# Idle products ahead of the first weights, an earlier split of the first weight, and three modulation steps taken behind the recurrence

## The chip, the cores and the metric

The kernel runs on one core of one Trainium2 chip. The metric is device microseconds (us) of one execution. The kernel before takes 2224.59 us, the median of 3 runs (2222.05 to 2225.04).

## What is computed

Two blocks of layers on 256 tokens, in fp32, with D = 1024. The first has an RG-LRU layer, a convolutional feed-forward, a stick-breaking attention and a second feed-forward, each followed by a layer norm:

```python
def rg_lru_block(x, w_in, b_in, conv_w, conv_b, w_gates, b_gates, a_param, w_out, b_out):
    proj = x @ w_in + b_in
    y_br = jax.nn.gelu(proj[..., :LRU_WIDTH])
    x_br = causal_depthwise_conv(proj[..., LRU_WIDTH:], conv_w, conv_b)
    ...
    _, h = lax.associative_scan(_lin_combine, (a, u), axis=1)
    return (h.astype(x.dtype) * y_br) @ w_out + b_out
...
        x = layer_norm(DN_ALPHA * x + mix, ln_g[layer, 0], ln_b[layer, 0])
        f = conv_ffn(x, ffn_w_up[layer], ffn_conv_w[layer], ffn_conv_b[layer], ffn_w_down[layer])
        x = layer_norm(DN_ALPHA * x + f, ln_g[layer, 1], ln_b[layer, 1])
```

The second block takes tokens and context through a Fourier and convolution mixer, attentions and two mixtures of experts, and ends in a norm. Its norms are scaled and shifted by a modulation that depends on neither block's tokens: silu(c) @ mod_w for two vectors c, of 6144 columns per layer and two layers. So the modulation can be computed at any time before the mixer.

## The kernel before

Activations lie transposed, 128 features on the partitions and eight chunks of 256 tokens behind each other. All weights stream from memory through a ring of 1 MB tiles (five of them in the first block), by DMAs that SyncE (SP) issues in the order of use (`start` and `load` in `run`); a tile's slot is free for the next when both of its halves have been used.

An fp32 product is made of three in a faster format. A weight piece is split by `cut`: ScalarE (ACT) copies it to `wh` (L382), VectorE (DVE) makes the rest `wl = w - wh` (L383). The tokens are split likewise into `xh` and `xl` (`parts`, in `begin` of `_first_block`: four quarters, L396 on ACT). TensorE (PE) then runs 8 x 3 products of 128 by 256 per piece: `wh` with `xh` (L405), `wh` with `xl` (L406), `wl` with `xh` (L407). Pieces are split up to four ahead of their products (`SPLITS`); a step of kind "ahead", which `K.ahead(n)` adds, makes the loop split up to n pieces beyond those already used.

The program is a list of steps that `run` carries out in order; each engine's queue has its instructions in that order. In `_lru` the order is: four pairs of signal products with the convolution behind them (`signal`, taps on DVE and GpSimd, POOL), with the small DVE instructions of `rates` (L711 to L730) behind the first pair; gates; four pairs of branch products with `decay`, `recur` (the scan) and `finish` between them. `finish(q)` is, for a quarter of the features, the Gelu (`yb`, L802, ACT), its product with the scan's result (`gi`, L806, DVE), and the split of that into `xbh` (L807, ACT) and `xbl` (L813, DVE). Behind `finish(3)` comes the output projection (`_block_out`, four pairs, accumulators `acc`), whose sums DVE adds to x (L692), and then the first layer norm: four centrings (DVE, L507, 512 columns each), their squares (ACT, L551) and column sums (PE, L564), the sum read by ACT (L571), a root, four scalings.

Two lists of steps wait at the side, a heavy one and a light one. `fill()` stands at numbered spots of the program, and takes from each list as many steps as the digit of `HEAVY` or `LIGHT` at that spot says, as far as there are any. Spot 2 is between the third pair with `finish(1)`, `finish(2)` and `finish(3)`; 4 to 7 lie in the output projection, 8 to 17 in the first layer norm (before it, after each centring, the root and each scaling), 18 to 53 in the first feed-forward, 54 to 63 in the second layer norm, and from 142 on in the mixer.

The light list holds the 48 modulation steps (`_modulation`, `one(g, k)`), each with a weight tile of 1 MB of its own, `mod_w`, used unsplit. A step is four products (L1082; eight records in the trace). The first step also sets up `sc`, silu of the two vectors (a memset on DVE, two Silus on ACT, L1076 and L1077). Every eighth step ends a group: a copy from PSUM on ACT (L1086), four transposes on PE (L1089), two additions on DVE (L1093). `LIGHT` has 48 in all.

`warm(n)` issues n products of 128 by 256 in bf16 whose result nobody reads.

Of the kernel before, what the change touches and what calls it, by code (L numbers as in the profile page):

```python
# [21 lines left out]
KC = D // P  # L22
# [131 lines left out]
class _K:  # L154
# [126 lines left out]
    def fill(self):  # L281

        for kind, table in ((self.heavy, HEAVY), (self.light, LIGHT)):
            n = int(table[self.spot]) if self.spot < len(table) else 0
# [110 lines left out]
    def parts(self, h, l, src):  # L395
        self.nc.scalar.activation(h, src, AF.Copy)  # L396
        self.nc.vector.tensor_sub(l, src, h)
# [57 lines left out]
            v.scalar_tensor_tensor(y, w, b, y, op0=ALU.add, op1=ALU.mult)  # L455
        return y

    def warm(self, n):

        w = self.cst[:, :256].bitcast(mybir.dt.bfloat16)  # L460
        ps = self.pt()[:, :w.shape[1]]
        for _ in range(n):
            self.nc.tensor.matmul(ps, lhsT=w[:, :P], rhs=w, start=True, stop=True)
# [76 lines left out]
class _Rms:  # L540
# [37 lines left out]
    def root(self, warm=0):  # L578
        ss = self.total() if self.ss is None else self.ss
        self.d = self.K.diagonal(self.K.inverse_root(ss[:, :, 0], [(2, self.n * P)], self.eps))  # L580
        self.K.warm(warm)
# [61 lines left out]


WARM = [8, 4, 4, 6]
HEAVY = "0000000000000100000000000000000000010101001000110000000000022001000001000000301000000010000000100001000100000000001000010000000000000000010000131301010000000000008110024100000000000"
LIGHT = "0000001101020010310001000110302000001010100100110100000500000000000000000100000000000000000100100000000000000000000000000000000000000001000011001001110000110000000001020300000000000"


class _Box:  # L650
# [392 lines left out]
def _first_block(K, X):  # L1043
    def begin():
        X.new("xh", [P, KC, T], F32R)
        X.new("xl", [P, KC, T], F32R)
        for q in range(0, KC, 2):
            K.parts(X.xh[:, q:q + 2], X.xl[:, q:q + 2], K.x[:, q:q + 2])
    K.add(begin)
    xh, xl, sy = (lambda: X.xh), (lambda: X.xl), (lambda: X.sy)  # L1050
    _lru(K, X)
    K.add(lambda: K.enter("cx", "right"))
    K.layer_norm(sy, 0, xh, xl)
    _ffn(K, 0, X)
    K.layer_norm(sy, 1, xh, xl)
    _stick(K, X)
    K.layer_norm(sy, 2, xh, xl)
    sums = _TwoNorms(K, 3)
    K.add(lambda: K.enter("two"))
    K.add(sums.prepare)  # L1060
    _ffn(K, 1, X)
    K.layer_norm(sy, 3, None, None, sums)
    K.add(lambda: K.leave("two"))
    return sums
# [37 lines left out]
def _modulate(K, src, l, r, which, gain, pool, parts=None, out=None, tmp=None, rms=None):  # L1102
# [10 lines left out]
    def first():  # L1113
# [3 lines left out]
        if summed:  # L1117
            rms.root(WARM[0])
            return
# [14 lines left out]
    def scale(k0):  # L1134
        def fn():
            if k0 == 0:
                box["r"] = rms.row()
                if summed:
                    K.warm(WARM[1])
            ks = range(k0, k0 + 4)  # L1140
# [532 lines left out]
class _Moe:  # L1673
# [87 lines left out]
    def experts(self, i, rms=None, side=None, tail=None):  # L1761
# [453 lines left out]
        self.tokens(i, "moe", ("xg", "yh"), keep=True, rms=rms, then=route, spare=spare)  # L2215
        K.add(lambda: K.warm(WARM[2]))
        K.add(places)
        K.add(lambda: K.warm(WARM[3]))
        if l == 0:
# [46 lines left out]
def _kernel(ctx, tc, a):  # L2266
# [12 lines left out]
    K.add(lambda: K.leave("rt"), K.heavy)  # L2279
    K.add(lambda: K.enter_ring(4), K.heavy)  # L2280
    sums = _first_block(K, X)
    K.add(lambda: K.leave("big"))
    K.add(lambda: K.enter("mx"))
# [41 lines left out]
```

## Time and profile before

| | |
|---|---|
| median of 3 runs | 2224.59 us (2222.05 to 2225.04) |
| profiled execution, time | 2220.28 us |
| profiled execution, span | 2218.5 us |
| mean granted clock of PE | 0.962 |
| PE busy (15884 products) | 1938.9 us, 87% |
| PE loading weights | 1445.7 us, 65% |
| DVE busy | 1060.0 us, 48% |
| ACT busy | 751.1 us, 34% |
| POOL busy | 450.4 us, 20% |
| moved by DMA | 603.15 MB, 272 GB/s on the mean |

The trace is of one execution, with times from the start of its span. A busy time is the time in which an engine runs an instruction, loads and waits apart. The granted clock is a share of full speed, taken for a stretch. An idle time before an instruction is followed by what ended it.

### The profile page before, as it was taken

Reading aid. Unit: us, or ns where it says so; the run is one execution under the profiler, and the core shown is the slowest. Engines: PE = TensorE matmul, PEld = TensorE weight load, DVE = VectorE, ACT = ScalarE, POOL = GpSimd, SP = SyncE. Lnnn points to the kernel's source line nnn. Section 1 sums busy time; section 2 is a strip of 40 time slices with the busy share of each in tenths; the row PEclk is TensorE's granted clock in tenths of the full one; section 3 lists DMA queues with packets and bytes.
Section 4 is the critical chain, followed back from the end, with each engine's and each line's share of the span. In section 5 each row is a group of like instructions: output and inputs, shape, how many; then the busy total and the mean of one; then the engine's idle time right before and its main releaser. Section 6 shows DMA issues by size and latency. Waiting matters only on the chain. (4 is left out here: it accounts for less than half of the span.)

```text
span 2218.5 us, 39754 instructions
## 1 busy us (share of the span) xinstructions
PE 1938.9 (87%) x15884; PEld 1445.7 (65%) x15884; DVE 1060.0 (48%) x1974; ACT 751.1 (34%) x1347; POOL 450.4 (20%) x496
## 2 busy tenths in 40 slices
PE   7889999998889998788989988898999887787875
PEld 6768997987789976665555455554877543343442
DVE  7665673576557568742333333335554322122222
ACT  5544653463446446431111111113444211111111
POOL 4122430799964206300000000001000000000000
PEclk9899999999999999999999999998999999999899
DMA  6477656534345544468999699992223899999995
GB/s 237 174 300 269 232 207 240 213 136 152 114 158 185 188 173 171 153 247 347 401 411 401 250 394 418 408 417 90 79 95 152 323 417 417 418 418 418 418 417 218
DMA packets 86458, 603.15 MB, mean 272 GB/s; under 512 B 9632, under 2 KB 12064, under 8 KB 13856
## 3 DMA queue, kind: packets, MB, share of 16 engines
q1 hardware_dynamic: 86176, 599.24, 68.2%
q8 instruction: 196, 3.21, 0.6%
q14 instruction: 86, 0.70, 0.1%
HBM read 598.15 MB, written 1.05 MB: 270 GB/s over the span
## 5 line engine op out<-in xcount | busy, mean ns | idle before, releaser
L405 PE MATMUL mm<-xh,wh 128*128 128x256 f32 x1024 | 296.3, 289 | 19.8 <-ACT wh L382 15.9
L407 PE MATMUL mm<-xh,wl 128*128 128x256 f32 x1024 | 294.1, 287 | 8.0 <-DVE wl L383 7.0
L406 PE MATMUL mm<-xl,wh 128*128 128x256 f32 x1024 | 294.4, 287 | 0.6 <-DVE xl L480 0.2
L1965 PE MATMUL acc<-down,hT 128*64 128x512 f32 x1024 | 255.6, 607 | 10.3 <-DMA down<-in_down_dram 4.5
L405 PEld LDWEIGHTS mm<-xh,wh 128*128 128x128 f32 x1024 | 200.3, 196 | 30.3 <-ACT wh L382 17.0
L407 PEld LDWEIGHTS mm<-xh,wl 128*128 128x128 f32 x1024 | 200.2, 196 | 9.6 <-DVE wl L383 8.4
L1910 DVE TENSOR_TENSOR hs<-hs,acc 128x128 f32<-128x128 f32 x81 | 23.3, 288 | 377.8 <-ACT hs L1909 363.7
L406 PEld LDWEIGHTS mm<-xl,wh 128*128 128x128 f32 x1024 | 200.4, 196 | 1.8 <-DVE xl L480 1.8
L2017 PE MATMUL acc<-gu,xc 128*32 128x256 f32 x2240 | 144.6, 394 | 61.3 <-DMA gu<-in_gu_dram 41.6
L2017 PE MATMUL acc<-gu,xg 128*32 128x256 f32 x2944 | 179.5, 394 | 20.5 <-PEq L2125 8.9
L1965 PEld LDWEIGHTS acc<-down,hT 128*64 128x64 f32 x1024 | 83.4, 139 | 159.8 <-issue 137.9
L2017 PEld LDWEIGHTS acc<-gu,xg 128*32 128x32 f32 x2944 | 111.6, 113 | 84.7 <-issue 36.3
L2017 PEld LDWEIGHTS acc<-gu,xc 128*32 128x32 f32 x2240 | 74.2, 112 | 127.2 <-DMA gu<-in_gu_dram 60.2
L1958 DVE SCALAR_TENSOR_TENSOR yl<-acc,wsl,yh 128x512 fp32r<-128x512 f32 x64 | 48.1, 751 | 208.6 <-ACT yh L1957 194.1
L1909 ACT ACTIVATE hs<-acc 128x128 f32<-128x128 f32 x81 | 22.4, 277 | 362.2 <-PE acc L2017 358.5
L383 DVE TENSOR_TENSOR wl<-ffn_w_up,wh 128x1024 fp32r<-128x1024 f32 x96 | 130.4, 1383 | 28.6 <-ACT wh L382 28.4
L405 PE MATMUL mm<-hh,wh 128*128 128x256 f32 (+1 forms) x416 | 128.5, 309 | 8.7 <-DVE cv L1250 5.9
L882 DVE SCALAR_TENSOR_TENSOR hv<-mm,vec,hv 128x255 f32<-128x255 f32 x192 | 88.2, 480 | 85.0 <-ACT hv L877 80.9
L406 PE MATMUL mm<-hl,wh 128*128 128x256 f32 (+1 forms) x416 | 124.1, 298 | 0.7 <-DVE hl L480 0.4
L407 PE MATMUL mm<-hh,wl 128*128 128x256 f32 (+1 forms) x416 | 123.6, 297 | 0.4 <-DVE wl L383 0.3
L1957 ACT ACTIVATE yh<-acc,wsl 128x512 fp32r<-128x512 f32 x64 | 44.0, 687 | 218.3 <-PE acc L1965 218.3
L424 POOL TENSOR_TENSOR xc<-xc,tot 128x256 f32<-128x256 f32 x4 | 2.9, 728 | 561.5 <-ACT tot L421 561.5
(496 smaller groups left out, 4479.6 us busy)
## 6 DMA issues: line engine op xcount, KB each, us to landing
gu<-in_gu_dram SPq DMA_DIRECT2D x256, 1024.0 KB, 18.3
down<-in_down_dram SPq DMA_DIRECT2D x128, 1024.0 KB, 17.3
mod_w<-in_mod_w_dram SPq DMA_DIRECT2D x48, 1024.0 KB, 4.8
ffn_w_up<-in_ffn_w_up_dram SPq DMA_DIRECT2D x48, 1024.0 KB, 4.9
ffn_w_down<-in_ffn_w_down_dram SPq DMA_DIRECT2D x24, 1024.0 KB, 4.9
w_in_ab<-in_w_in_ab_dram SPq DMA_DIRECT2D x12, 1024.0 KB, 4.8
kv_w<-in_kv_w_dram SPq DMA_DIRECT2D x8, 1024.0 KB, 6.9
w_out_ab<-in_w_out_ab_dram SPq DMA_DIRECT2D x8, 1024.0 KB, 4.8
```

What stands on the lines that cost most here:

```text
L383: self.lows.append(lambda: nc.vector.tensor_sub(wl, src, wh))
L405: mm(out, lhsT=wh(k), rhs=xh(k), start=s, stop=False, **kw)
L406: mm(out, lhsT=wh(k), rhs=xl(k), start=False, stop=False, **kw)
L407: mm(out, lhsT=wl(k), rhs=xh(k), start=False, stop=e, **kw)
L424: eng.tensor_tensor(out, out, t, op=ALU.add)
L882: nc.vector.scalar_tensor_tensor(hv[:, s, d:], ps[:, s * T:(s + 1) * T - d], cw(2 - d, m), hv[:, s, d:], op0=ALU.mult, op1=ALU.add)
L1909: nc.scalar.activation(hs, gu[:, 0:P], AF.Silu)
L1910: nc.vector.tensor_mul(hs, hs, gu[:, P:2 * P])
L1957: nc.scalar.activation(yh, ps, AF.Identity, scale=wsl)
L1958: nc.vector.scalar_tensor_tensor(yl, ps, wsl, yh, op0=ALU.mult, op1=ALU.subtract)
L1965: mm(ys[n][64 * s:64 * s + 64], lhsT=hT[:, at(c)], rhs=part(ws[s], c)[:, n * 512:n * 512 + 512], start=c == 0, stop=c == 3, tile_position= ...
L2017: mm(out[c], lhsT=lhsT, rhs=rhs(q), tile_position=(0, LOT * q), skip_group_check=True, **kw)
```

## The change

`LIGHT` has a 3 at spot 2 in place of a 0: the first three modulation steps, with the set-up of `sc`, are taken behind `finish(2)`. As the table has 51 then and there are 48 steps, each later spot takes steps that stand three further in the list, and the last spot (169) takes none of the three that it took. In `_first_block` only the first quarter of x is split ahead of the first weight piece; `K.ahead(1)` splits that piece next, and the other quarters follow. Ahead of all this stand 40 idle products (`FIRST`), whose operand is the constant matrix of ones read as bf16, which `warm` now takes as an argument. Line numbers grow by 2 to 8 with it.

```diff
--- before.py
+++ after.py
@@ -455,9 +455,9 @@
             v.scalar_tensor_tensor(y, w, b, y, op0=ALU.add, op1=ALU.mult)
         return y
 
-    def warm(self, n):
-
-        w = self.cst[:, :256].bitcast(mybir.dt.bfloat16)
+    def warm(self, n, src=None):
+
+        w = (self.cst[:, :256] if src is None else src).bitcast(mybir.dt.bfloat16)
         ps = self.pt()[:, :w.shape[1]]
         for _ in range(n):
             self.nc.tensor.matmul(ps, lhsT=w[:, :P], rhs=w, start=True, stop=True)
@@ -643,8 +643,10 @@
 
 
 WARM = [8, 4, 4, 6]
+
+FIRST = 40
 HEAVY = "0000000000000100000000000000000000010101001000110000000000022001000001000000301000000010000000100001000100000000001000010000000000000000010000131301010000000000008110024100000000000"
-LIGHT = "0000001101020010310001000110302000001010100100110100000500000000000000000100000000000000000100100000000000000000000000000000000000000001000011001001110000110000000001020300000000000"
+LIGHT = "0030001101020010310001000110302000001010100100110100000500000000000000000100000000000000000100100000000000000000000000000000000000000001000011001001110000110000000001020300000000000"
 
 
 class _Box:
@@ -1044,9 +1046,15 @@
     def begin():
         X.new("xh", [P, KC, T], F32R)
         X.new("xl", [P, KC, T], F32R)
-        for q in range(0, KC, 2):
-            K.parts(X.xh[:, q:q + 2], X.xl[:, q:q + 2], K.x[:, q:q + 2])
+        K.warm(FIRST, K.ones)
+        parts(0)
+
+    def parts(q):
+        K.parts(X.xh[:, q:q + 2], X.xl[:, q:q + 2], K.x[:, q:q + 2])
     K.add(begin)
+
+    K.ahead(1)
+    K.add(lambda: [parts(q) for q in range(2, KC, 2)])
     xh, xl, sy = (lambda: X.xh), (lambda: X.xl), (lambda: X.sy)
     _lru(K, X)
     K.add(lambda: K.enter("cx", "right"))
```

How the instructions move is shown at three places. The first is ACT's queue behind the recurrence, from the third `xbh` back; before:

```order
L807 ACTIVATE xbh<-gi 128x512
L382 ACTIVATE wh<-lru_w_out 128x1024
L795 ACTIVATE yb<-mm,vec_87 128x256
L802 ACTIVATE yb<-yb 128x512
L807 ACTIVATE xbh<-gi 128x512
L802 ACTIVATE yb<-yb 128x512
L807 ACTIVATE xbh<-gi 128x512
L382 ACTIVATE wh<-lru_w_out 128x1024 x5
L1076 ACT_TABLE_LOAD
L1076 ACTIVATE sc<-vec_87 128x8
L1077 ACTIVATE sc<-vec_87 128x8
```

The changed kernel has there:

```order
L809 ACTIVATE xbh<-gi 128x512
L382 ACTIVATE wh<-lru_w_out 128x1024
L797 ACTIVATE yb<-mm,vec_87 128x256
L804 ACTIVATE yb<-yb 128x512
L809 ACTIVATE xbh<-gi 128x512
L1084 ACT_TABLE_LOAD
L1084 ACTIVATE sc<-vec_87 128x8
L1085 ACTIVATE sc<-vec_87 128x8
L804 ACT_TABLE_LOAD
L804 ACTIVATE yb<-yb 128x512
L809 ACTIVATE xbh<-gi 128x512
L382 ACTIVATE wh<-lru_w_out 128x1024 x5
```

The two Silus stand between the third and the fourth quarter, with a table load before them and one behind.

The second place is PE's queue at the same spot, from the last branch products to the first output products (`mm` against `acc`); before:

```order
L405 MATMUL mm<-xh,wh 128x256
L406 MATMUL mm<-xl,wh 128x256
L407 MATMUL mm<-xh,wl 128x256
L405 MATMUL acc<-xbh,wh 128x256
L406 MATMUL acc<-xbl,wh 128x256
L407 MATMUL acc<-xbh,wl 128x256
```

In the changed kernel:

```order
L407 MATMUL mm<-xh,wl 128x256
L1090 MATMUL mod<-mod_w_492,sc 32x512 x4
L1090 MATMUL mod<-mod_w_537,sc 32x512 x4
L1090 MATMUL mod<-mod_w_616,sc 32x512 x4
L405 MATMUL acc<-xbh,wh 128x256
L406 MATMUL acc<-xbl,wh 128x256
```

All output products now stand behind the twelve of the three steps.

The third place is DVE's queue in the first layer norm, from the last output sum on; before:

```order
L692 TENSOR_TENSOR x<-x,acc 128x256
L221 TENSOR_REDUCE sel<-cst 128x1 x2
L507 SCALAR_TENSOR_TENSOR x<-mm,x 128x512 x4
L447 TENSOR_SCALAR ra<-mm 128x2
L449 TENSOR_SCALAR rw<-ra 128x2
```

In the changed kernel:

```order
L694 TENSOR_TENSOR x<-x,acc 128x256
L221 TENSOR_REDUCE sel<-cst 128x1 x2
L507 SCALAR_TENSOR_TENSOR x<-mm,x 128x512 x3
L1101 TENSOR_TENSOR mod_932<-mod,vec_87 128x16 x2
L507 SCALAR_TENSOR_TENSOR x<-mm,x 128x512
L447 TENSOR_SCALAR ra<-mm 128x2
```

The two additions that end the first group (`mod_932`) stand ahead of the fourth centring. In the second layer norm the second group's end stands in the same way behind the first centring.

## Rows read from the trace of the kernel before

**Rows 1.** Windows: stretch, length; busy us (count) of PE, PEld, DVE, ACT, POOL; clock, DMA share, GB/s.

```profile
10.62:17.17 6.55, 6.09 (x26) 5.79 (x27) 4.13 (x4) 3.24 (x4) 0.00 (x0) 1.00 1.03 421
17.17:25.00 7.83, 7.83 (x67) 7.83 (x67) 7.33 (x18) 4.70 (x9) 4.08 (x7) 1.00 1.01 421
88.00:92.00 4.00, 3.68 (x17) 3.39 (x17) 3.38 (x6) 2.18 (x3) 0.00 (x0) 0.50 0.00 0
92.00:94.00 2.00, 2.00 (x18) 2.00 (x17) 1.53 (x3) 0.46 (x1) 0.00 (x0) 0.92 0.88 262
```

**Rows 2.** Timeline of the front: start, length, engine, line, operation, count [idle before <- what ended it].

```profile
10.62 0.58 PE L405 MATMUL mm<-xh,wh 128*128 128x256 f32 x1 [10.62 <-ACT wh L382]
...
14.38 2.00 ACT L382 ACTIVATE wh<-lru_w_in 128x1024 fp32r<-128x1024 f32 x2 [2.57 <-DMA lru_w_in<-in_lru_w_in_dram]
...
15.47 2.36 DVE L383 TENSOR_TENSOR wl<-lru_w_in,wh 128x1024 fp32r<-128x1024 f32 x2 [2.41 <-ACT wh L382]
...
28.81 0.62 DVE L730 TENSOR_SCALAR bg<-vec 128x16 f32<-128x16 f32 x1
...
29.35 1.21 DVE L383 TENSOR_TENSOR wl<-lru_w_in,wh 128x1024 fp32r<-128x1024 f32 x1
...
30.61 0.39 PE L407 MATMUL mm<-xh,wl 128*128 128x256 f32 x1 [1.75 <-DVE wl L383]
```

**Rows 3.** Timeline, recurrence and output projection, and the first modulation step.

```profile
71.08 1.28 ACT L802 ACT_TABLE_LOAD   x1
...
72.38 0.63 ACT L802 ACTIVATE yb<-yb 128x512 f32<-128x512 f32 x1
...
79.33 0.63 ACT L807 ACTIVATE xbh<-gi 128x512 fp32r<-128x512 f32 x1 [6.32 <-DVE gi L806]
...
80.01 0.58 PE L405 MATMUL acc<-xbh,wh 128*128 128x256 f32 x1 [3.37 <-ACT xbh L807]
...
86.33 0.63 ACT L807 ACTIVATE xbh<-gi 128x512 fp32r<-128x512 f32 x1 [1.07 <-DVE gi L806]
...
88.86 0.58 PE L406 MATMUL acc<-xbl,wh 128*128 128x256 f32 x1 [0.32 <-DVE xbl L813]
...
94.86 0.42 DVE L692 TENSOR_TENSOR x<-x,acc 128x256 f32<-128x256 f32 x1 [0.88 <-PE acc L407]
...
108.91 0.20 ACT L1077 ACTIVATE sc<-vec 128x8 f32<-128x8 f32 x1
...
109.16 1.07 PE L1082 MATMUL mod<-mod_w,sc 128*32 128x512 f32 x8 [0.70 <-ACT sc L1077]
```

**Rows 4.** Timeline, second layer norm.

```profile
376.32 4.50 PE L1082 MATMUL mod<-mod_w,sc 128*32 128x512 f32 x40
...
383.21 0.38 ACT L571 ACTIVATE tot<-mm 128x256 f32<-128x256 f32 x1 [0.73 <-PE mm L564]
```

**Rows 5.** Timeline, mixer and its end.

```profile
855.40 0.66 PE L1089 MATMUL mod<-cst,sq 128*128 128x128 f32 x4 [2.68 <-ACT sq L1086]
...
949.69 2.78 PE L1082 MATMUL mod<-mod_w,sc 128*32 128x512 f32 x24
...
953.20 0.65 PE L1089 MATMUL mod<-cst,sq 128*128 128x128 f32 x4 [0.72 <-ACT sq L1086]
```

**Rows 6.** Timeline, first layer norm.

```profile
118.70 2.48 DVE L507 SCALAR_TENSOR_TENSOR x<-mm,x 128x512 f32<-128x512 f32 x4 [1.50 <-PE mm L698]
...
121.16 1.89 PE L1082 MATMUL mod<-mod_w,sc 128*32 128x512 f32 x14
...
123.53 0.38 ACT L571 ACTIVATE tot<-mm 128x256 f32<-128x256 f32 x1 [1.47 <-PE mm L564]
...
133.23 0.57 ACT L1086 ACTIVATE sq<-mod 128x512 f32<-128x512 f32 x1
...
134.55 0.26 DVE L1093 TENSOR_TENSOR mod<-mod,vec 128x16 f32<-128x16 f32 x2 [0.71 <-PE mod L1089]
```

**Rows 7.** The page: DVE's busy tenths in 40 equal slices of the span.

```profile
DVE  7665673576557568742333333335554322122222
```

## The prediction

> **What bounds the kernel now.** I read the stretches by window first, then the order of time around the three places that the diff touches, then the places to which the change pushes other work. The front: TensorE (PE) has nothing to do until 10.62 us, and its first 26 products take 6.55 us, where 67 take 7.83 us right behind [rows 1]. That is 0.25 against 0.117 us each: the lower of the clock's two levels (1.2 GHz), then 2.4 GHz; the granted clock reads 1.00 in both, so the spacing tells it. But PE is not what the front waits for. VectorE (DVE) gets its third set of low parts at 15.47 us, because ScalarE (ACT) waited 2.57 us for that weight tile's DMA, and from there it runs without a gap: two low parts, the first convolution, one low part, then the small instructions of `rates`, the last at 28.81 us, and the low part of the sixth group at 29.35 us [rows 2]. PE stands 1.75 us for that one before 30.61 us [rows 2].
>
> Behind the recurrence PE is idle for 3.37 us before the first output product at 80.01 us, then works in short pieces as the merged quarters come, until the last wait at 88.86 us [rows 3]. There its clock is at 0.50, and it reaches 0.92 in the next two microseconds [rows 1].
>
> **The change, part by part.**
> *Front: 0 (from -1 to +1).* Idle products and the earlier split let PE start about a microsecond sooner and at 2.4 GHz: 26 x (0.25 - 0.117) = 3.5, with the start some 4 us of PE time. The cover is DVE. Nothing ahead of 15.47 us on its queue feeds on PE, the DMA that sets 15.47 us is issued in the same place, and its queue up to 29.35 us has the same instructions in the same order. So the sixth group still gets its low part at about 30.6 us; PE waits 5 us there and not 1.75, and goes cold as before. What may shift is how GpSimd's (POOL's) taps fall against DVE's instructions, hence the microsecond either way.
>
> *Output projection: +3.8 (+2.0 to +5.4).* This is the main cost. The three steps now stand on PE between the last branch product and the first output product, and the first of them sets up `sc`: a memset, a table load for Silu, and two Silus behind the third `xbh` on ACT. That `xbh` starts at 86.33 us and lasts 0.63 [rows 3]. A table load is 1.28 us, and its user begins 0.02 later [rows 3]; the two Silus (0.20 long for the second, before 109.16 us) end 0.3 behind that [rows 3]. So PE gets `sc` at about 88.6 us, and everything behind it in PE's queue, 19 output products that ran in the gaps before, waits too. A step is eight records, 1.07 us alone [rows 3], 0.86 in a row: (4.50 - 2.78) / 2 between forty records and twenty-four [rows 4, 5]. PE has then been idle for 12 us. Before, work from 88.86 us on ran at 0.50 until about 92.3, that is 3.4 us [rows 1, 3]; taking the same, two steps run at 1.72 and the third at 0.86, to 92.9. Two output groups are 48 products of 0.117, to 98.6, where DVE took the second at 94.86 [rows 3]: +3.8. Bounds: full clock from the start gives +2.0; the 6.55 us of half clock at the front gives 1.6 more than taken, +5.4. The second load, back to Gelu, delays the last quarter to about 92.6, which PE needs only after 18 of those products: nothing.
>
> The Trainium skill (ScalarE: Activation LUTs, What ACT_TABLE_LOAD costs) puts a switch at about 2.66 us, a drain being added to the load. Rows 3 have 1.28 and no gap, and the row decides. By the page this term would be 1.4 more and the sum 8.2.
>
> *The step in the seventh group: -0.7.* PE waited 0.70 for `sc` before 109.16 us [rows 3]; it is there already.
>
> *The weights' DMAs: 0.* Three mod tiles take the ring slots in which output weights lay; those are issued two slots later. The first lands about a microsecond late, where ACT waits some 6 us anyway (6.32 before 79.33 us) [rows 3]; the others land before their split. SP gains no waits elsewhere: the same slots come free by the same steps, three loads on.
>
> *Every eighth step moves.* A group's end is a copy on ACT (0.57), four transposes on PE (0.65), two additions on DVE (0.26) [rows 5, 6]. Steps are still taken at the same later places, three steps on, so these ends land elsewhere.
> - First layer norm, +3.1 (+2 to +4). The end comes after the second step there, ended at 121.16 + 1.89 = 123.05, and DVE's additions stand ahead of the fourth centring. The four centrings took 2.48 in one piece from 118.70 [rows 6]. Now: copy to 123.7, transposes to 124.4, additions to 124.7, centring 0.62 to 125.3, square 0.63 to 126.0, its products (four records, as the transposes) to 126.6; ACT then reads the sum, which it did at 123.53 [rows 6].
> - The same layer norm's second half, -1.0: the copy (0.57) and DVE's wait of 0.71 with the additions leave the last scaling [rows 6]. PE then stands some 2.4 us before the feed-forward; if its clock falls, +1.3; I take half, +0.6.
> - Second layer norm, +2.5 (+1.5 to +3.5). Five steps run there from 376.32; the end comes after the fourth, 379.9, ahead of three centrings. Additions end at 381.6; the fifth step and the products that free the square buffer at 383.2; three squares and the last products at 385.7; ACT read the sum at 383.21 [rows 4].
> - Feed-forward, third layer norm: 0. The ends shift between places where PE pays the same wait.
> - Mixer, +1.2 (-1.9 to +1.4). An end comes into PE's run of products at 820 us: 0.72 + 0.65 [rows 5]. It leaves 855.40, where PE waited 2.68 [rows 5]; but DVE is busy 8 tenths of that slice, its densest [rows 7], so I give back 0.2 and keep 3.3 as the bound.
> - Mixer's end, -2.7 (-4.1 to 0). Three steps and the end leave 949.69: 2.78 + 0.72 + 0.65 [rows 5]. The end now sits before 937, behind eight copies on ACT, and holds a norm's row until about 942: DVE's `cv` chain is 2.7 later, half of which PE's idle ahead of the first output products hides. 4.1 - 1.4.
>
> **Sum:** 0 + 3.8 - 0.7 + 3.1 - 1.0 + 0.6 + 2.5 + 1.2 - 2.7 = **+6.8 us**. All places but the front lie on a path with no cover behind it: expert weights are prefetched only a few tiles deep, so the streams start that much later. The profiled execution took 2220.28, so 2227.1; the median of the runs is 4.3 higher, 2224.59, and the forecast for a median is **2231.4**.
>
> **Rivals.**
> *The front's gain arrives* (not slower). If DVE's stretch to 29.35 shortens with POOL's taps drawn forward, or the sixth group's wait doesn't end last, PE's 4 us pass: +2.8, 2227.4, within the bound. It decides from the point where the low part of that group is ready before 26 us. Against it: DVE's rows touch. The Trainium skill (TensorE: Matmul & The Clock Gate, Why this matters for your kernels) advises sustained work to reach the full clock; rows 1 agree on the 2:1, and by that rule alone the front would be worth these 4 us. Chance 0.13.
> *The group ends in the layer norms are hidden* by waits that I missed: 6.8 - 5.6, 2225.8, no change. Against it: DVE's queue has the additions in the middle of the centrings. 0.10.
> *The clock stays low longer*, behind the 12 us gap and at the feed-forward: +1.6 + 0.7, 2233.7. 0.12.
> *The idle products don't raise the clock* (half their operand's values are zeros): the front is hidden, so the forecast stands.
> The forecast itself: 0.57; for what I don't see, 0.08, mostly of a gain.
>
> **Numbers.** No change is what a measurement of this kernel can't tell apart, 0.2% or 4.4 us. Of the forecast's 0.57 a fifth lies under that by its bounds; with the low-clock case, slower 0.56. The two hidden cases and that fifth: same 0.34. Faster needs the front, the mixer's bounds and something more: 0.10. The range leaves out a tenth on each side: 2225 to 2237.
>
> **What would show it.** In the changed profile: PE products well before 10 us and none slow at the front, but the product that waits for `wl` still near 30.6; a wait of PE for `sc` near 88.6 and mod records of about 1 us length behind it; DVE's output sums 3 to 5 us later; the first norm's sum read 3 us further behind its centring; five steps and an end in the second. I am wrong if DVE's `wl` of the sixth group comes before 28 us, or if the output projection starts on time.

## The result and the profile after

The changed kernel takes 2233.41 us, the median of 6 runs (2230.60 to 2237.55), against 2221.94 us of the kernel before (6 runs, 2216.50 to 2225.04). The ratio is 1.0061, with a 95% interval of 1.0046 to 1.0076: slower by 13.5 us of 2222 (10 to 17); the two medians lie 11.47 us apart. The forecast was slower, by 6.8 us: the sign is right, the size is half of what the ratio gives. The profiled executions stand further apart than the medians: 2234.63 against 2220.28 us, 14.4 us.

Timeline of the changed kernel, front and output projection (columns as in [rows 2, 3]; line numbers are 2 to 8 higher than there; here and below other rows stand between the rows shown):

```profile
1.06 5.89 PE L463 MATMUL mm<-ones 128*128 128x256 bf16 x40 [1.06 <-DVE ones L189]
...
30.14 1.22 DVE L383 TENSOR_TENSOR wl<-lru_w_in,wh 128x1024 fp32r<-128x1024 f32 x1
31.41 0.58 PE L407 MATMUL mm<-xh,wl 128*128 128x256 f32 x1 [5.75 <-DVE wl L383]
...
86.81 0.63 ACT L809 ACTIVATE xbh<-gi 128x512 fp32r<-128x512 f32 x1 [1.07 <-DVE gi L808]
87.45 1.28 ACT L1084 ACT_TABLE_LOAD   x1
88.74 0.21 ACT L1084 ACTIVATE sc<-vec 128x8 f32<-128x8 f32 x1
88.86 0.20 ACT L1085 ACTIVATE sc<-vec 128x8 f32<-128x8 f32 x1
89.07 1.28 ACT L804 ACT_TABLE_LOAD   x1
89.11 4.50 PE L1090 MATMUL mod<-mod_w,sc 128*32 128x512 f32 x24 [11.99 <-ACT sc L1085]
93.54 0.39 PE L405 MATMUL acc<-xbh,wh 128*128 128x256 f32 x1
99.60 0.42 DVE L694 TENSOR_TENSOR x<-x,acc 128x256 f32<-128x256 f32 x1 [0.42 <-PE acc L407]
```

The front is there: idle products from 1.06 us, and the first real one comes at 7.13 us in place of 10.62. All of it is given back by 31.41 us, most of it at one row: PE waits 5.75 us for the sixth group's low part, 1.75 before [rows 2], and DVE starts that part 0.8 us later than before. Behind the recurrence PE stands 11.99 us for `sc`, and the three steps take 4.50 us.

The layer norms of the changed kernel, with the ends of the first two groups in them:

```profile
122.65 1.89 DVE L507 SCALAR_TENSOR_TENSOR x<-mm,x 128x512 f32<-128x512 f32 x3 [1.50 <-PE mm L700]
127.11 0.60 ACT L1094 ACTIVATE sq<-mod 128x512 f32<-128x512 f32 x1 [1.70 <-PE mod L1090]
127.76 0.66 PE L1097 MATMUL mod<-cst,sq 128*128 128x128 f32 x4 [0.76 <-ACT sq L1094]
128.45 0.26 DVE L1101 TENSOR_TENSOR mod<-mod,vec 128x16 f32<-128x16 f32 x2 [3.91 <-PE mod L1097]
128.62 0.68 DVE L507 SCALAR_TENSOR_TENSOR x<-mm,x 128x512 f32<-128x512 f32 x1
131.19 0.38 ACT L571 ACTIVATE tot<-mm 128x256 f32<-128x256 f32 x1 [1.15 <-PE mm L564]
...
388.50 0.26 DVE L1101 TENSOR_TENSOR mod<-mod,vec 128x16 f32<-128x16 f32 x2 [4.25 <-PE mod L1097]
388.68 1.88 DVE L507 SCALAR_TENSOR_TENSOR x<-mm,x 128x512 f32<-128x512 f32 x3
392.26 0.38 ACT L571 ACTIVATE tot<-mm 128x256 f32<-128x256 f32 x1 [0.73 <-PE mm L564]
```

DVE waits 3.91 and 4.25 us in the middle of the centrings, and the sums are read 7.66 and 9.05 us later than in [rows 6] and [rows 4]. Now the mixer's end, first in the kernel before:

```profile
934.34 1.92 PE L1082 MATMUL mod<-mod_w,sc 128*32 128x512 f32 x16
936.24 0.70 PE L586 MATMUL mm<-rd,ones 128*128 128x256 f32 x2
937.17 3.76 PE L1726 MATMUL mm<-rw,h2T 128*128 128x36 f32 x32 [0.23 <-ACT h2T L1149]
939.24 0.47 DVE L1250 SCALAR_TENSOR_TENSOR cv<-cv,vec,mm 128x256 f32<-128x256 f32 x1
945.83 1.55 ACT L1739 ACTIVATE h2h<-acc 128x512 fp32r<-128x512 f32 x3
```

and in the changed kernel, with two windows (columns as in [rows 1]) behind the rows:

```profile
940.11 1.22 DVE L383 TENSOR_TENSOR wl<-w_out_ab,wh 128x1024 fp32r<-128x1024 f32 x1
942.02 1.28 DVE L1247 TENSOR_TENSOR cv<-cv,cg 128x512 f32<-128x512 f32 x2
945.14 0.38 ACT L571 ACTIVATE tot<-mm 128x256 f32<-128x256 f32 x1 [1.17 <-PE mm L564]
947.58 3.64 PE L1090 MATMUL mod<-mod_w,sc 128*32 128x512 f32 x16
949.33 3.30 ACT L1157 ACTIVATE h2T<-mt,mod 128x256 f32<-128x256 f32 x8 [3.80 <-DVE mt L1156]
952.53 0.57 ACT L1094 ACTIVATE sq<-mod 128x512 f32<-128x512 f32 x1
953.16 1.12 PE L1097 MATMUL mod<-cst,sq 128*128 128x128 f32 x4 [1.94 <-ACT sq L1094]
954.07 1.06 PE L586 MATMUL mm<-rd,ones 128*128 128x256 f32 x2
954.92 6.88 PE L1734 MATMUL mm<-rw,h2T 128*128 128x36 f32 x32
955.17 0.48 DVE L1258 SCALAR_TENSOR_TENSOR cv<-cv,vec,mm 128x256 f32<-128x256 f32 x1 [0.60 <-PE mm L586]
962.74 0.60 ACT L1747 ACTIVATE h2h<-acc 128x512 fp32r<-128x512 f32 x1 [0.96 <-PE acc L1745]
...
936.00:944.00 8.00, 5.07 (x40) 3.63 (x40) 6.37 (x15) 3.35 (x6) 2.86 (x4) 0.91 0.58 217
944.00:966.00 22.00, 19.58 (x89) 14.80 (x86) 10.92 (x33) 9.99 (x23) 0.00 (x0) 0.50 0.30 107
```

The end of the group (L1094, L1097) waits for the eight copies `h2T` on ACT. Behind its transposes on PE stand the row of a norm (`mm<-rd,ones`), for which DVE's `cv` chain waits, and the router's 32 products (`mm<-rw,h2T`). Where the norm's sum (`tot`) comes 12.31 us later than before, `cv` begins 15.93 later, the router's products 17.75, and `h2h`, the first copy behind the router, 16.91; the clock reads 0.50 from 944 to 966 us.

The lag of the changed kernel behind the one before, from the starts of the same instruction in both traces, and what each piece adds, beside the forecast:

| up to | lag, us | added | forecast |
|---|---|---|---|
| third `xbh`, 86.33 before | 0.48 | 0.5 | 0 |
| second output sum, 94.86 | 4.74 | 4.3 | 3.8 |
| first centring, 118.70 | 3.95 | -0.8 | -0.7 |
| first norm's sum, 123.53 | 7.66 | 3.7 | 3.1 |
| sum ahead of the second norm, 279.03 | 7.13 | -0.5 | -0.4 |
| second norm's sum, 383.21 | 9.05 | 1.9 | 2.5 |
| fourth norm's sum, 540.12 | 9.06 | 0 | 0 |
| mixer's sum, 924.77 | 10.73 | 1.7 | 1.2 |
| first small copy of the routing (`d`), 988.07 | 13.21 | 2.5 | -2.7 |
| end of the span | 14.4 | 1.2 | 0 |

### The profile page after: what moved, and what is told of

The parts are those of the page before. It is cut to its first block, busy times and chain, and to the rows that moved or that the text cites. A ratio compares the mean times of both kernels' runs of the same rounds, so it can differ in the third digit from the quotient of the medians.

```text
span 2232.9 us, 39843 instructions
## 1 busy us (share of the span) xinstructions
PE 1958.5 (88%) x15918; PEld 1454.8 (65%) x15924; DVE 1059.6 (47%) x1974; ACT 751.9 (34%) x1347; POOL 451.5 (20%) x496
## 5 line engine op out<-in xcount | busy, mean ns | idle before, releaser
L2025 PE MATMUL acc<-gu,xc 128*32 128x256 f32 x2240 | 149.8, 408 | 56.0 <-DMA gu<-in_gu_dram 29.7
L382 ACT ACTIVATE wh<-ffn_w_up 128x1024 fp32r<-128x1024 f32 x96 | 101.0, 1055 | 44.9 <-PE mm L406 16.5
```

Of the source, the lines that this page charges most:

```text
L382: nc.scalar.activation(wh, src, AF.Copy)
L2025: mm(out[c], lhsT=lhsT, rhs=rhs(q), tile_position=(0, LOT * q), skip_group_check=True, **kw)
```

## The experiments

Each ratio is to the kernel before, run beside it on the same chip. Beside the total, the starts of landmarks are compared with the profile of before: up to 540 us they repeat well from kernel to kernel, while the total of one execution varies by more (the 23 runs of before on one chip went from 2213.68 to 2225.41 us).

**1. The front alone.** `LIGHT` as before.

> The front of the change alone (idle products, first piece split behind the first quarter); LIGHT as before. Theory: DVE covers it. The low part of the sixth group still starts near 30 us (29.35 before, 30.14 with the whole change), and the time is that of before, +0.5 us (-1 to +1.5). Rival: the front does give or cost time by itself: 4 us less (PE's products at 2.4 GHz from the start), or more than 3 us more, which would mean that part of the 11.5 us of the whole change comes from there.

Ratio 1.0011 (1.0000 to 1.0023), medians 2222.62 and 2220.41 us. The lag is 0.81 us at the last `xbh`, 0.82 at the first norm's sum, and still 0.84 at 988 us. Most of the front is found in one wait:

```profile
31.16 0.58 PE L407 MATMUL mm<-xh,wl 128*128 128x256 f32 x1 [5.77 <-DVE wl L383]
```

DVE's low part covers it, as forecast. Against the expectation the median is a little high (2.2 us where -1 to +1.5 was given), with an interval that reaches 0. That the 0.8 us are the front's is not shown: run 2, which has the front of before, starts the same low part 0.86 us late as well.

```profile
30.21 1.21 DVE L383 TENSOR_TENSOR wl<-lru_w_in,wh 128x1024 fp32r<-128x1024 f32 x1
```

**2. The three steps alone.** `begin` as before, `LIGHT` of the change.

> The three modulation steps alone; front as before. Theory: this is the whole of the slowdown: +11 us over before (+8 to +13). Rival: the two parts act on each other (PE comes to the steps earlier or later by the front), and this alone is +6 or less.

Ratio 1.0062 (1.0044 to 1.0079): as slow as the whole change, 13.8 us, a little over the range. The lag is 7.79 at the first norm's sum and 9.17 at the second's, as in the whole change. So the steps alone give the whole slowdown, within the intervals; the rival falls.

**3. The ends of the groups put back.**

```diff
-LIGHT = "0030001101020010310001...
+LIGHT = "0030000000020010310001...
```

> The whole change, but the digits of three single steps at spots 6, 7 and 9 (two in the output projection, one in the first layer norm) are 0, so that from the norm's second centring on every modulation step and every group end stands where it stood before. Theory: more than half of the cost is that the ends of the groups land in the layer norms and at the mixer's end: the output projection keeps its +4.8 us less the 0.7 us wait and the one or two us of the two steps taken from it, and all the rest goes: +2 us over before (0 to +4); the sum of the first norm is read 4 us sooner behind its centrings than in the changed kernel, and the clock at the mixer's end is 1.00 again. Rival: what is late behind the output projection is a result of starting late (weights, clock), not of the ends: +8 us or more.

Ratio 1.0029 (1.0017 to 1.0041), 6.4 us: between the theories. The norms are settled: the first centring lags 1.96 us and the norm's sum 1.95, so the 3.7 us are gone; so is the second norm's cost (1.44 and 1.45 on both sides), and at 540 us the lag is 0.82. At the mixer's end the norm's sum and the first `h2h` behind the router lag alike (5.52 and 5.53), where the changed kernel goes from 12.31 to 16.91. So the 4.6 us of delay there come with the end's place too. The low part `wl` at 940 us is not there either. But this execution lost 4.2 us between 540 and 828 us, where its instructions stand in the same order as before. About 2.0 of them go between 791 and 802 us (times before), at a norm; the clock of a window just behind its sum reads 0.72 here and 1.00 before. This run's window comes first, then that of before:

```profile
801.00:813.00 12.00, 11.21 (x57) 6.31 (x58) 7.77 (x34) 4.36 (x11) 0.23 (x2) 0.72 0.44 160
798.00:810.00 12.00, 9.98 (x65) 6.06 (x66) 9.47 (x39) 5.45 (x13) 0.23 (x2) 1.00 0.65 256
```

The parts of the theory on the norms and on the delay at the mixer's end are shown; its total is not. The clock at the mixer's end is not all 1.00 again, as was expected: it reads 0.79 from 936 to 944 us, and nothing is late by that.

**4. `sc` early.** On top of the change:

```diff
     def begin():
+        K.sc = K.tile("wp", [P, KC, 32], F32, "sc")
+        nc.gpsimd.memset(K.sc, 0.0)
...
             nc.scalar.activation(B.a2[:, sl], B.a2[:, sl], AF.Sqrt)
+            if hf == 1:
+                nc.scalar.activation(K.sc[:, :, 0], K.v("c_2", 0, 8), AF.Silu)
+                nc.scalar.activation(K.sc[:, :, 1], K.v("c_ctx_2", 0, 8), AF.Silu)
```

> The whole change, but `sc` is made early: its memset on GpSimd at the start of the RG-LRU layer, its two Silus on ACT behind the second half's square root, ahead of the first Gelu, where ACT waited over 5 us for the scan. Theory: PE stands for `sc` and not for the steps; the 24 records of the three steps then run from about 77 us in the gap ahead of the first output product, and the output projection starts at 80 us as before: 4 to 5 us less than the changed kernel, +7 us over before (+5 to +9). Rival: the steps' own time costs, wherever they stand behind the branch products (4.5 us of PE): +10 us or more.

```profile
77.63 2.78 PE L1091 MATMUL mod<-mod_w,sc 128*32 128x512 f32 x24
80.40 0.63 ACT L814 ACTIVATE xbh<-gi 128x512 fp32r<-128x512 f32 x1 [4.70 <-DVE gi L813]
81.08 0.38 PE L405 MATMUL acc<-xbh,wh 128*128 128x256 f32 x1 [0.67 <-ACT xbh L814]
```

The 24 records take 2.78 us in the gap, at the higher clock, and the first centring lags 0.39 us in place of 3.95. So PE stood for `sc`, and the steps cost nothing there. The total is 1.0047 (1.0031 to 1.0063), 10.4 us, more than expected, and by itself it would fit the rival (10 or more); it is the landmark that decides. The norms still add 3.3 and 1.9 us, and this execution too lost 4.7 us between 540 and 828.

**5. Both: `sc` early, ends in their places.**

> The two edits before together: the changed kernel with `sc` made early and with the digits at spots 6, 7 and 9 at 0, so that the ends of the groups stand where they stood. Theory: then nothing of the slowdown is left, and the two steps taken from the output projection (1.07 us each) come for nothing in the gap ahead of it: the first norm's sum 1.5 to 2 us sooner than before, and -3 us over all (-5 to +2, the upper end if the second feed-forward and the mixer lose the 4 us again that they lost in the run with the ends put back). Rival: modulation steps that early cost by themselves (their weights push others back): +3 us or more over before, already at the first norm.

Ratio 0.9997 (0.9986 to 1.0008). The first norm's sum comes 2.38 us sooner than before, and the fourth norm's 3.02; the profiled execution then loses 4.4 us up to 828 us. Nothing of the slowdown is left, and no gain in the total can be told from none. The rival, by which steps that early cost by themselves, falls.

**6. Short `rates`, front of before.** The 25 DVE instructions of the polynomial are out and `na` is made from `t2`. With it the values differ, other experts get other tokens, and the total (0.9925) cannot be compared; only times ahead of the routing are read.

> The kernel before, with the polynomial in `rates` left out (the log1p of the decay rates, some 20 small DVE instructions; the output is not the reference's). Theory: DVE sets when the sixth group's low part is there; it comes 5 us or more sooner, PE's wait of 1.75 us goes and so does the half clock behind it: -3 us (-5 to -1). Rival: it is ACT or the weights' DMA that holds the sixth group, and DVE only follows: within 1 us of before.

PE no longer waits for the sixth group, so DVE held it; the first centring comes 1.13 us sooner, less than thought. The next wait grew in its place, ahead of the gates:

```profile
41.82 0.58 PE L405 MATMUL mm<-xbh,wh 128*128 128x256 f32 x1 [3.53 <-ACT gi L751]
```

**7. The same with the front of the change.**

> The same omission (the polynomial in `rates`), with the front of the change: idle products, first piece split early; LIGHT as before. Theory: with the cover gone the front is worth the 3.5 us that PE's slow products took: 3 to 4 us less than the kernel with the short `rates` alone, -6 us over before. Rival: the front is worth nothing, cover or not (PE waits in other places, at 16 us and at the gates): within 1 us of the kernel with the short `rates`.

The first centring comes 1.51 us sooner than before, 0.4 better than without the front. The theory, 3 to 4 us, falls and its rival, within 1 us, holds. What now covers the front, on PE, on ACT and on POOL:

```profile
42.96 0.58 PE L405 MATMUL mm<-xbh,wh 128*128 128x256 f32 x1 [6.59 <-ACT gi L753]
```

```profile
41.19 0.42 ACT L742 ACTIVATE xbh<-xb 128x256 fp32r<-128x256 f32 x1 [5.50 <-POOL xb L424]
```

```profile
25.48 0.72 POOL L732 TENSOR_SCALAR xb<-pj,vec 128x256 f32<-128x256 f32 x1
...
33.18 2.83 POOL L732 TENSOR_SCALAR xb<-pj,vec 128x256 f32<-128x256 f32 x1
...
40.52 0.63 POOL L424 TENSOR_TENSOR xb<-xb,tap 128x253 f32<-128x253 f32 x1
```

Read in this order: PE waits for a Tanh on ACT, that stands behind an `xbh` for which ACT waits 5.50 us, and POOL, without a pause since 18.95 us, ends the convolution at 41.15.

**8. A whole kernel with early `rates`.** To run 5's `LIGHT` and `sc`, with the front of before:

```diff
     K.add(begin)
+    K.ahead(2)
+    K.add(rates)
     for ci in range(4):
         K.addw("lru_w_in", 4 + ci, signal(ci))
-        if ci == 0:
-            K.add(rates)
```

> A whole kernel: the front as before; all of `rates` on DVE between the second and the third low part, where it waits 2.4 us for a weight; LIGHT with the three steps early and the ends in their places; `sc` early. Theory: the gains of the two parts add: -6 us over before (-9 to -2). Rival: the third low part, about 3 us later, stops PE at 20 us: -1 us or worse.

Ratio 0.9996 (0.9984 to 1.0008). The first centring comes 2.53 us sooner, what run 5 has already (2.38), though run 5 has the front of the change and this one that of before: early `rates` add nothing that shows, and PE now waits 6.14 us ahead of the gates. The theory (-9 to -2) falls. This execution lost nothing between 540 and 828 us (-2.48 and -2.73).

**9. Idle products at the mixer's end.** On top of the change, in `gather` of the mixer: `if to is None: K.warm(24, K.ones)`.

> The changed kernel with 24 idle products of 128 by 256 on PE at the mixer's end, in the 2.9 us in which PE waits (from 940.5 us) for the squares of `cv`. Theory: what ate the gain there is the clock: in the changed kernel it reads 0.50 from 944 to 966 us and the sixteen records of two modulation steps take 3.64 us instead of 1.92, the router's 32 products 6.88 instead of 3.76. Kept at work, PE stays at 1.00 there, the first h2h comes 3 to 5 us sooner, and the whole is 2 to 4 us under the changed kernel (+8 to +11 us over before). Rival: the clock falls all the same, or what it costs is hidden by the chain on DVE and ACT: the time of the changed kernel, +12 to +14.

Ratio 1.0079 (1.0063 to 1.0094): no gain.

```profile
947.79 1.92 PE L1090 MATMUL mod<-mod_w,sc 128*32 128x512 f32 x16
953.89 0.83 PE L1097 MATMUL mod<-cst,sq 128*128 128x128 f32 x4 [4.18 <-ACT sq L1094]
955.37 6.88 PE L1736 MATMUL mm<-rw,h2T 128*128 128x36 f32 x32
```

The two steps ran at the higher clock (1.92 us in place of 3.64), and PE then waited 4.18 us in place of 1.94 for the copy of the group's end, and the router's products took 6.88 us all the same. Runs 2 and 4, without idle products there, have the same 1.92 us, so the idle products need not have made the difference. In all three `h2h` still comes 3.9 to 4.2 us later behind the norm's sum than before (4.6 in the changed kernel). The clock of the two steps was not the cause: the end's copy, behind eight others on ACT, sets when PE goes on.

**10 and 11. Both covers away.** Short `rates`, and `for s in ((1, 2, 3) if h == 0 else ())` in `signal`: POOL's taps for the odd halves are left out. Run 10 has the front of before, run 11 that of the change. One execution each, read ahead of the routing.

> The kernel before without the polynomial in `rates` and without the three taps of the odd halves on GpSimd (the convolution of four of eight feature chunks is left out; the output is not the reference's, and the experts' stage is not comparable, so only times up to the first norm are read). Theory: behind DVE stood GpSimd; without its taps PE's wait for `xbh` (3.5 us in the run with short `rates`) goes, and the first centring comes 4 to 6 us sooner than before. Rival: DVE's own taps for the even halves hold the gates just as long: the first centring within 1 us of the run with short `rates` (-1.1 us).

> The same omissions with the front of the change. Theory: with both covers gone, the front's earlier and faster products arrive: the first centring 3 to 4 us sooner than in the run with the same omissions and the front of before. Rival: a third cover (the weights' DMA, ACT, DVE's taps) hides it again: less than 1 us.

The first centring comes 6.76 us sooner than before in run 10, more than the 4 to 6 expected (PE's wait ahead of the gates is 0.99 us), and 9.69 in run 11. So POOL was the second cover; with both gone the front is worth 2.93 us, just under what was expected.

**12. Idle products ahead of the gates.** On top of run 8: `K.add(lambda: K.warm(50, K.ones))` ahead of the gates' first products.

> The kernel with early `rates`, the ends in their places and `sc` early, and 50 idle products ahead of the gates, where PE waits 6 us (38.7 to 44.8 us) for GpSimd's part of the convolution and its clock falls to 0.50 from 41 to 48 us. Theory: the clock stays at 1.00, some 3 us of products at half clock are saved behind the wait, PE is the bound from there to the last branch product at 73 us: the first centring 1.5 to 3 us sooner than without them, the whole -4 us against before (-6 to -1). Rival: the scan's chain on DVE and ACT sets the start of the output projection: no gain over the same kernel without them (-0.9 us against before).

The place itself did as expected: no half clock from 41 to 48 us, and the first centring 4.62 us sooner than before, 2.1 better than run 8; at 999 us it is 7.46 ahead. But the total is 1.0013 (1.0004 to 1.0023), 2.9 us slower than before. The profiled execution is the fastest of the twelve (2216.72 us, the median 2221.87), so it doesn't show what the others lose. Even there 5.5 us of the lead go between 999 and 1261 us, in the experts' stage. Other profiles change there too, run 9 by 4.1 us the other way. Why is open; no run here tells.

No whole kernel of these beats the one before; runs 5 and 8 equal it, and so beat the changed one.

## Why the forecast was right, and where it was not

*Front.* Right in size and cause (forecast 0, range -1 to +1; run 1 gives 0.8, but run 2, without the front, has its low part as late). The low part came near 30 us, as said, and DVE is the cover. The rival by which the gain arrives is out. What the text did not see is a second cover behind the first, POOL's taps: shortening `rates` doesn't free the front (run 7), taking both covers does (run 11). The 0.25 us per product that it read at the front hold waits as well: single products there start 0.213 us apart, and 0.12 behind, so that the clock alone is 26 x 0.093 = 2.4 us and not 3.5. In the changed kernel products start 0.12 us apart from 8.6 us on, behind the 40 idle ones. The advice of the Trainium skill (TensorE: Matmul & The Clock Gate, Why this matters for your kernels), to keep TensorE busy for the full clock, is borne out by that; it was worth nothing here because of the two covers.

*Output projection.* Right by mechanism and size: `sc` at 89.1 us (said 88.6), 4.50 us of steps (said 4.3), the second sum 4.3 us later behind the recurrence's own 0.5 (said 3.8). Run 4 shows that it is the wait for `sc`. (The 19 products that it has in the gaps before are 13 in the trace; the sum doesn't use them.) The table load is 1.28 us, without a gap of more than 0.02 us before or behind it, both ways, so the row was the right price. The Trainium skill (ScalarE: Activation LUTs, What ACT_TABLE_LOAD costs) gives 2.66 us for a switch, load and drain together; the load agrees, a drain doesn't show in this trace.

*Layer norms.* 3.7 and 1.9 us against 3.1 and 2.5: the sum of the two is right, and run 3, in which both go, shows the ends to be the cause. The rival by which they are hidden is out. The second half's -1.0 and +0.6 are not worked out to the end from rows; together they are -0.4, and the trace has -0.5.

*Mixer.* The 1.7 us of the table agree with 1.2 by luck, since single executions vary by more here. But the end that moves into PE's products does show: between 820 and 829 us (times before) the lag grows by 1.28 us in the changed kernel and as much in runs 2, 4 and 9, and not at all in runs 1, 3, 5 and 8.

*Mixer's end, the term that failed.* The forecast took -2.7 there, and the trace has +2.5, which is 5.2 of the 7.6 us between 6.8 and 14.4. Runs 2, 4 and 9, with the same ends, have +1.1, +1.2 and +1.0, so that its sign is wrong in all four profiles. What is given back behind was right: 3.7 us (16.91 to 13.21) here and 4.1 to 4.2 in the others, where 4.1 was forecast; but runs with the ends in their places also vary there, from -1.7 to +1.5. What failed is the delay ahead of it, 1.4 in "DVE's `cv` chain is 2.7 later, half of which PE's idle ahead of the first output products hides". Nothing is hidden. Behind the norm's sum the `cv` chain is 3.6 us later (15.93 against 12.31; 2.9 to 3.2 in the other three), since PE's row for it stands behind the transposes, and they behind ACT's copies. `h2h` is 1.0 later still, as it waits for PE, whose router products take 6.88 us in place of 3.76. And 1.1 us come ahead of the norm's sum, in all four, from a low part (`wl`, 940.11 us) that stands on DVE ahead of the sums of `cv`; before, it came behind the router. The forecast has no such term, and why that split moves is not shown.

That the delay goes with the end's place is shown by run 3. How much of it is half clock is not; an estimate from the rows is the last wait, 0.96 us, with 0.47 for the transposes (1.12 in place of 0.65 us) and 0.36 for the row (1.06 in place of 0.70).

*The rest.* The experts' stage, taken at nothing, adds 1.2 us in this pair of profiles, within what single executions vary by. The median's 11.5 us lie 2.9 under the profiles' 14.4.

*What was luck.* The forecast for the median, 2231.4, is only 2.0 us from the 2233.41 measured, but it was added to 2224.59, the median of three runs of before; six runs give 2221.94, and from there the forecast would have been 2228.7. That the low-clock case (2233.7) meets the number is luck too. Behind the gap for `sc` the clock was 0.85 already from 92 to 94 us, as the forecast itself had taken it. At the feed-forward it did fall (0.66 from 130 to 145 us, 1.00 before), but the lag shrank there by 0.5. The low clock at the mixer's end it didn't name.

## What to carry to other kernels

A step moved by a count in a schedule moves every periodic piece behind it: look up where each group's end lands, and follow what stands behind it on *each* engine (here from ACT to PE to DVE), before you take any of it as hidden. A set-up that a moved step brings along (here two Silus and two table loads) can cost more than the step; made where its engine waits anyway, it freed the 3.6 us. Before an engine's early start is paid for, count the covers: remove one in an experiment, and see whether the next wait takes its place.

## What was not expected of the hardware

The same instruction on POOL, `xb<-pj` of 128 by 256, took 0.72 and 2.83 us in run 7, at 25.48 and 33.18 us. During the long one DVE made two low parts (from 33.39 us, 1.21 us each); it was busy during the short one too, and what makes the difference is not shown. Idle products in bf16, with half of their operand's values zero, were enough for the higher clock at the front.

The stretch from 540 to 828 us, with its instructions in unchanged order, took 4.2 to 4.4 us longer in the profiles of runs 3 and 5 and no longer in those of runs 1, 8 and 12. Some 2.0 us of it are lost at one norm: in runs 2, 3, 4 and 5 the clock of the 12 us just behind its sum reads 0.72, and in the kernel before, the changed one and runs 1 and 8, which lose nothing there, 1.00. What decides where the clock falls is open. So a single profile's lag past 540 us is not to be read closer than some 4 us; what several profiles with the same order show alike, as at the mixer's end, can be.
